# A two-layer SSM, Fourier and attention backbone: the second layer's rotations go from GpSimd to VectorE

## The chip, the core and the metric

The kernel runs on one core of a Trainium2 chip. The core has TensorE for matmuls (PE in the profile), VectorE (DVE), ScalarE (ACT), GpSimd (POOL) and SyncE (SP), each with an instruction queue of its own that it works off in order; they meet through semaphores. Measured is the time of one execution on the device, in microseconds (us); a kernel's time is the median of its runs.

## What is computed

Two layers; each mixes 512 latent tokens and 256 context tokens by three heads side by side (a complex state-space model, a Fourier mixer, a windowed attention with rotary embedding), with one projection in and one out, and then runs a gated FFN. Cut to what the change touches:

```python
h = modulate(rmsnorm(x, g_pre_mix), sh1, sc1) @ w_in
u, f, q, k, v = jnp.split(h, splits, axis=-1)
y_ssm, yc_ssm = s5_mixer(u, uc, ...)       # for both directions: h_t = lam * h_(t-1) + B u_t, lam complex
y_fft = fnet_mixer(f, w_fourier)
q = axial_rope(q); k = axial_rope(k)       # x1*cos - x2*sin, x2*cos + x1*sin
y_na = na_latent(q, k, v, kc, vc, rpb)
o = jnp.concatenate([y_ssm, y_fft, y_na], axis=-1) @ w_out
x = x + g1 * rmsnorm(o, g_post_mix)
x = x + g2 * rmsnorm(swiglu(modulate(rmsnorm(x, g_pre_ffn), sh2, sc2), ...), g_post_ffn)
```

## The kernel before

Almost all of the time is matmuls in split precision: a float32 operand is cut into a high part (a copy on ACT, L584) and a low part (a subtraction on DVE, L565), and three products are summed (L593, L641, L859, L864, L1181). The stages of a layer follow each other; inside the mixing stage they are woven.

**The state-space stage.** `ssm` runs twelve steps k (six groups of heads, two directions each). Step k has two halves. `ssm_scan` multiplies the step's input by a table on PE (L725, four matmuls into PSUM), turns the result by a rotation on DVE (three products and a sum, L280, read from PSUM), runs four real scans on DVE (L735), and turns the result back: three products with the cosine and sine parts of the step's table (L738 to L740), a small memset (L743 or L746), and a difference (L744 in even steps, L747 and L748 in odd ones). `ssm_out` multiplies the outcome on PE (L760, and L762 in odd steps, which close a group) and applies a GELU by ACT and DVE (L283, whose output tile is `z`). L757 opens the PSUM tile of a group. The table `tab` of a step has three buffers; the table of step k+3 is loaded (L507, from SP's queue) once step k's last product, L740, has read its own. In the first layer the tables are built while the stage runs; in the second they are loaded ready-made.

**What is woven with it.** The chunks of the input projection (L593), named u0 to u2, k0, q0, k1, q1, k2, q2, f0, f1; each q and k chunk goes through `rope`: a copy by ACT (L697), a shuffle on DVE (L698), a product with the sine table (L699), a product with the cosine table and a sum (L280 on the `s` tiles). Then the values' projection (L641) and the Fourier mixer (L849, L859, L864). After the last step the attention starts (`attn`, first scores on PE at L985): it loads keys (L936) and queries (L935) through DMAs on POOL's queue. The queries go into a buffer `u` that held tables of the state-space steps, so this load waits for the last `ssm_out` matmul (L762); the keys go into `tab` buffers. The softmax's first step on DVE is L1006.

**What sets the order.** The program is written as generators that are woven in fixed ratios. The framework then schedules: it assigns every instruction a place in its engine's queue, by its own estimate of when operands and buffers are ready. An instruction that goes to another engine therefore also moves its neighbours, on PE and in the DMA queue too.

In the first layer (`l == 0`) the products with the sine table and the turning back run on DVE, in the second on POOL.

Of the kernel before, what the change touches and what calls it, by code (L numbers as in the profile page):

```python
# [12 lines left out]
ALU = mybir.AluOpType  # L13
# [21 lines left out]
class Builder:  # L35
# [654 lines left out]
    def rope(self, l, dst, pl, pc, scale):  # L690
        nc = self.nc
        if self.rc is None:
            self.rc, self.rs = self.s(), self.s()
            nc.sync.dma_start(self.rc, self.ap["rope"][:, 0, :])
            nc.sync.dma_start(self.rs, self.ap["rope"][:, 1, :])
        q, sh = self.s(), self.s()
        nc.scalar.activation(q, pl, AF.Copy, scale=scale)  # L697
        nc.vector.stream_shuffle(sh, q, [(i + 16) % 32 for i in range(32)])  # L698
        (nc.vector if l == 0 else nc.gpsimd).tensor_tensor(out=sh, in0=sh, in1=self.rs, op=ALU.mult)  # L699
        self.tt(q, q, self.rc, ALU.mult)  # L700
        self.tt(q, q, sh, ALU.add)
        parts = [(q, 0, NL)]
        if pc is not None:
            qc = self.c()
            nc.scalar.activation(qc, pc, AF.Copy, scale=scale)
            parts.append((qc, NL, NT))
        for x, a, b in parts:
            new = self.s if a == 0 else self.c
            hl = (new(F32R), new(F32R))
            self.split(*hl, x)  # L710
            for i in range(2):
                nc.sync.dma_start(dst(i)[..., a:b], hl[i].bitcast(F32))


    def ssm_scan(self, l, k, tab):
        nc = self.nc
        u, d = k // 2, k % 2
        U = self.U[u // 2]
        tab = tab[0]
        bT = tab[:, 0:512].rearrange("p (g c) -> p g c", g=4)  # L720
        co = tab[:, 512:896].rearrange("p (g c) -> p g c", g=4)
        si = tab[:, 896:1280].rearrange("p (g c) -> p g c", g=4)
        sp = self.ps("a", [128, 4, 96])
        for i in range(4):
            nc.tensor.matmul(sp[:, i, :], bT[:, i, :], U[:, 4 * (u % 2) + i, 32 * d:32 * d + 96],  # L725
                             start=True, stop=True)
        src = sp if d == 0 else sp[:, :, ::-1]
        t1, t2, gg = (self.q(shape=(128, 4, 96)) for _ in range(3))
        self.tt(t1, src, co, ALU.mult)
        self.tt(t2[0:64], src[64:128], si[64:128], ALU.mult)  # L730
        self.tt(t2[64:128], src[0:64], si[0:64], ALU.mult)
        self.tt(t1, t1, t2, ALU.add)
        for i in range(4):
            j = k * 4 + i
            nc.vector.tensor_tensor_scan(gg[:, i, :], self.rho[l][:, j:j + 1].to_broadcast([128, 96]),  # L735
                                         t1[:, i, :], 0.0, op0=ALU.mult, op1=ALU.add)
        gp = nc.vector if l == 0 else nc.gpsimd
        gp.tensor_tensor(out=t1, in0=gg, in1=co, op=ALU.mult)  # L738
        gp.tensor_tensor(out=t2[0:64], in0=gg[64:128], in1=si[64:128], op=ALU.mult)
        gp.tensor_tensor(out=t2[64:128], in0=gg[0:64], in1=si[0:64], op=ALU.mult)  # L740
        hh = gg
        if d == 0:
            gp.memset(hh[:, :, 0:1], 0.0)  # L743
            gp.tensor_tensor(out=hh[:, :, 1:96], in0=t1[:, :, 0:95], in1=t2[:, :, 0:95], op=ALU.subtract)  # L744
        else:
            gp.memset(hh[:, :, 31:32], 0.0)  # L746
            gp.tensor_tensor(out=hh[:, :, 32:96], in0=t1[:, :, 94:30:-1], in1=t2[:, :, 94:30:-1], op=ALU.subtract)  # L747
            gp.tensor_tensor(out=hh[:, :, 0:31], in0=t1[:, :, 30::-1], in1=t2[:, :, 30::-1], op=ALU.subtract)  # L748
        return hh
# [703 lines left out]
```

## Time and profile before

| | us |
|---|---|
| median of the 3 runs shown | 1658.99 |
| lowest and highest of them | 1652.31, 1659.48 |
| the profiled execution | 1655.93 |
| its span, first to last instruction | 1654.1 |
| PE busy | 1588.4 (96%) |
| DVE busy | 996.6 (60%) |
| POOL busy | 237.2 (14%) |
| second layer's state-space stage, from first L725 to first L985 | 1060.87 to 1171.64 |

The profile is one execution. Each row of its views gives times from the start of the span. "Idle before" is the time for which an engine had nothing to run ahead of an instruction, and the arrow names what ended it. A busy PE is not a PE at its peak; its granted clock is given beside it, 1.00 for 2.4 GHz and 0.50 for 1.2 GHz.

### The profile page before, as it was taken

To read this page: it belongs to the slowest core of one execution; us is meant where nothing else is said; L and a number is where in the kernel's file an instruction comes from. 1 tells how busy PE (TensorE), PEld (TensorE's weight loads), DVE (VectorE), ACT (ScalarE), POOL (GpSimd) and SP (SyncE) were. 2 spreads that over 40 slices of the span, in tenths; PEclk is the share of its full clock that TensorE was granted. 3 is DMA by queue.
4 is the path that set the end of the run, shared out by engine and by line. 5 is a ranking of instruction groups with operands and counts; after the bars stand their busy time and mean duration, and the time that the engine had idled before them with its cause. 6 is when DMAs were issued, how large, how long until landed. Compare 5 with 4: busy or idle time off the path is not lost. (4 is left out here: it accounts for less than half of the span.)

```text
span 1654.1 us, 23548 instructions
## 1 busy us (share of the span) xinstructions
PE 1588.4 (96%) x9097; PEld 1305.8 (79%) x9097; DVE 996.6 (60%) x1891; ACT 651.9 (39%) x1241; POOL 237.2 (14%) x266
## 2 busy tenths in 40 slices
PE   5999689999999999999999999989999999999997
PEld 1887676678988888778788788879777888888886
DVE  7699986765565666433343357697764534554455
ACT  6546545646556322211121138322554432222222
POOL 1000022002111224000000014375411100000002
PEclk8999899999999999999999999999899999999999
DMA  8444377634133424632524356476724422233222
GB/s 319 157 151 137 93 213 240 234 129 166 58 126 117 147 92 140 218 142 90 191 99 149 126 185 207 159 227 198 222 65 140 133 87 100 77 119 103 84 80 86
DMA packets 101391, 240.08 MB, mean 145 GB/s; under 512 B 25424, under 2 KB 56784, under 8 KB 88480
## 3 DMA queue, kind: packets, MB, share of 16 engines
q1 hardware_dynamic: 97968, 229.93, 41.3%
q0 software_dynamic: 3312, 8.65, 1.7%
q8 instruction: 71, 1.16, 0.3%
q14 instruction: 40, 0.33, 0.1%
HBM read 201.26 MB, written 38.47 MB: 145 GB/s over the span
## 5 line engine op out<-in xcount | busy, mean ns | idle before, releaser
L593 PE MATMUL b<-s,wh 128*128 128x512 f32 (+1 forms) x1856 | 551.0, 376 | 1.6 <-DVE s L565 0.6
L593 PEld LDWEIGHTS b<-s,wh 128*128 128x128 f32 x1856 | 337.8, 189 | 74.5 <-issue 9.8
L593 PE MATMUL b<-s,wl 128*128 128x512 f32 (+1 forms) x928 | 345.8, 374 | 1.6 <-DVE wl L565 1.6
L584 ACT ACTIVATE wh<-wr 128x1024 fp32r<-128x1024 f32 (+4 forms) x184 | 185.3, 1027 | 341.8 <-PE b L593 248.2
L565 DVE TENSOR_TENSOR wl<-wr,wh 128x1024 fp32r<-128x1024 f32 (+4 forms) x184 | 221.1, 1217 | 110.0 <-ACT wh L584 100.4
L280 DVE TENSOR_TENSOR q<-q,b 128x512 f32<-128x512 f32 x180 | 122.7, 684 | 165.6 <-PE b L1181 165.0
L593 PEld LDWEIGHTS b<-s,wl 128*128 128x128 f32 x928 | 175.0, 189 | 32.8 <-DVE wl L565 2.7
L593 PE MATMUL b<-c,wh 128*128 128x256 f32 x944 | 179.1, 284 | 0.0
L593 PEld LDWEIGHTS b<-c,wh 128*128 128x128 f32 x944 | 151.3, 191 | 5.5 <-issue 0.6
L283 DVE SCALAR_TENSOR_TENSOR s<-s,b 128x512 f32<-128x512 f32 x88 | 60.2, 685 | 134.2 <-PE b L593 87.0
L1181 PE MATMUL b<-wh,tab 128*128 128x512 f32 x400 | 136.9, 393 | 0.0
L593 PE MATMUL b<-c,wl 128*128 128x256 f32 x472 | 133.1, 284 | 0.0
L1181 PE MATMUL b<-wh,s 128*128 128x512 f32 x384 | 130.0, 392 | 0.0
L593 PEld LDWEIGHTS b<-c,wl 128*128 128x128 f32 x472 | 90.2, 191 | 1.4 <-issue 0.2
L1181 PEld LDWEIGHTS b<-wh,tab 128*128 128x128 f32 x400 | 75.0, 188 | 19.2 <-ACT c L1158 2.5
L1181 PEld LDWEIGHTS b<-wh,s 128*128 128x128 f32 x384 | 72.1, 188 | 19.9 <-issue 2.5
L1181 PE MATMUL b<-wl,tab 128*128 128x512 f32 x200 | 78.3, 392 | 0.0
L1181 PE MATMUL b<-wl,s 128*128 128x512 f32 x192 | 74.7, 390 | 0.0
L1213 POOL TENSOR_TENSOR q<-q,g 128x512 f32<-128x512 f32 x10 | 13.9, 1392 | 367.0 <-ACT junk L515 336.1
L584 ACT ACTIVATE s<-s 128x512 fp32r<-128x512 f32 x43 | 26.9, 627 | 92.2 <-DVE s L283 52.8
L527 POOL TENSOR_TENSOR ss<-ss,cols 128x1 f32<-128x1 f32 x42 | 30.3, 723 | 191.4 <-DVE ss L283 190.7
L1158 ACT ACTIVATE s<-b 128x512 f32<-128x512 f32 x44 | 25.9, 589 | 78.1 <-PE b L593 78.1
(325 smaller groups left out, 2615.6 us busy)
## 6 DMA issues: line engine op xcount, KB each, us to landing
wr<-in_w_gu SPq DMA_DIRECT2D x44, 1024.0 KB
wmod<-in_w_mod SPq DMA_DIRECT2D x46, 512.0 KB
wr<-in_w_down SPq DMA_DIRECT2D x22, 1024.0 KB
wmod<-in_w_mod SPq DMA_DIRECT2D x16, 1024.0 KB
wr<-in_w_in SPq DMA_DIRECT2D x10, 1024.0 KB
u<-in_w_mod SPq DMA_DIRECT2D x18, 512.0 KB
wr<-in_w_out SPq DMA_DIRECT2D x8, 1024.0 KB
tab<-tabd SPq DMA_DIRECT2D x12, 640.0 KB
```

The costliest lines, as they stand in the source:

```text
L280: self.nc.vector.tensor_tensor(out=out, in0=a, in1=b, op=op)
L283: self.nc.vector.scalar_tensor_tensor(out=out, in0=a, scalar=s, in1=b, op0=op0, op1=op1)
L527: nc.gpsimd.tensor_tensor(out=ss[:, 3:4], in0=ss[:, 2:3], in1=self.mhalf, op=ALU.pow)
L565: (eng or self.nc.vector).tensor_tensor(out=lo, in0=x, in1=hi.bitcast(F32), op=ALU.subtract)
L584: ins = self.nc.scalar.activation(hi, x, AF.Copy)
L593: self.nc.tensor.matmul(out, a[k], h[k][v][:, cs], start=(k == 0 and i == 0), stop=(k == 7 and i == 2))
L1158: nc.scalar.activation(tmp[v], gp, AF.Tanh, scale=0.5)
L1181: nc.tensor.matmul(pd, a[v][:, cs], w[:, ds], start=(j == 0 and i == 0), stop=(j == n - 1 and i == 2))
L1213: (nc.gpsimd, nc.vector)[hf].tensor_tensor(out=oo[hf], in0=oo[hf], in1=gates[t // 4][:, hf * 512:(hf + 1) * 512], op=ALU.mult)
```

## The change

Two expressions that choose the engine by the layer now choose VectorE in both. In the second layer six instructions of L699 and the twelve steps' L738, L739, L740, the memsets L743 or L746, and L744 or L747 and L748, move from POOL's queue to DVE's. What they compute, their tiles and the tiles' pools stay as they were.

```diff
@@ rope
-        (nc.vector if l == 0 else nc.gpsimd).tensor_tensor(out=sh, in0=sh, in1=self.rs, op=ALU.mult)
+        (nc.vector).tensor_tensor(out=sh, in0=sh, in1=self.rs, op=ALU.mult)
@@ ssm_scan
-        gp = nc.vector if l == 0 else nc.gpsimd
+        gp = nc.vector
         gp.tensor_tensor(out=t1, in0=gg, in1=co, op=ALU.mult)
         gp.tensor_tensor(out=t2[0:64], in0=gg[64:128], in1=si[64:128], op=ALU.mult)
         gp.tensor_tensor(out=t2[64:128], in0=gg[0:64], in1=si[0:64], op=ALU.mult)
```

The scheduler gives new places to the instructions around them, from the second layer's first steps up to the attention's first scores; behind that the queues are as before.

DVE, the last scan (k = 11, `q<-rho`) and what follows it up to the attention's first softmax step; `wl` are weights' low parts, 128x1024 those of the output projection, `c<-wr` those of the FFN. Before:

```order
L565 TENSOR_TENSOR wl<-wr,wh 128x768
L735 SCALAR_TENSOR_TENSOR q<-rho_146,q 128x96 x4
L565 TENSOR_TENSOR wl<-wr,wh 128x384
L283 SCALAR_TENSOR_TENSOR z<-q,b 128x384
L565 TENSOR_TENSOR s<-b,s 128x512 x4
L565 TENSOR_TENSOR c<-b,c 1x256
L565 TENSOR_TENSOR c<-wr,c 128x256 x3
L283 SCALAR_TENSOR_TENSOR q<-q,b 128x384
L565 TENSOR_TENSOR c<-wr,c 128x256 x2
```

And now:

```order
L565 TENSOR_TENSOR wl<-wr,wh 128x1024
L565 TENSOR_TENSOR c<-wr,c 128x256
L565 TENSOR_TENSOR wl<-wr,wh 128x1024
L283 SCALAR_TENSOR_TENSOR z<-q,b 128x384
L735 SCALAR_TENSOR_TENSOR q<-rho_146,q 128x96 x4
L738 TENSOR_TENSOR q<-q,tab 128x384
L739 TENSOR_TENSOR q<-q,tab 64x384
L740 TENSOR_TENSOR q<-q,tab 64x384
L746 MEMSET q 128x4
L747 TENSOR_TENSOR q<-q 128x4x64
L748 TENSOR_TENSOR q<-q 128x4x31
L565 TENSOR_TENSOR s<-s,u 128x512
```

The last scan has moved behind the Fourier mixer's splits (`s<-b,s`), the FFN's and two of the output projection's, and the turning back stands behind it on the same queue.

PE, from the last matmuls of the state-space stage to the first scores; L864 are 30 matmuls of the Fourier mixer. Before:

```order
L760 MATMUL b<-q,u 128x96
L762 MATMUL b<-U,q 128x96
L864 MATMUL b<-wh,s 128x260 x2
L864 MATMUL b<-wl,s 128x260
...
L864 MATMUL b<-wh,c 128x260 x2
L864 MATMUL b<-wl,c 128x260
L985 MATMUL b<-tab,u 128x256 x30
```

And now:

```order
L864 MATMUL b<-wh,c 128x260 x2
L864 MATMUL b<-wl,c 128x260
L757 LDWEIGHTS zero
L757 MATMUL b<-zero 128x384
L760 MATMUL b<-q,u 128x96 x5
L762 MATMUL b<-U,q 128x96
...
L760 MATMUL b<-q,u 128x96
L762 MATMUL b<-U,q 128x96
L985 MATMUL b<-tab,u 128x256 x24
```

The 30 matmuls stood between the last step's L762 and the first scores; now they stand ahead of the last two steps' `ssm_out`, and the scores follow L762 at once.

## Rows read from the trace of the kernel before

**Rows 1.** The page: busy time by engine; costliest groups (busy us, mean ns, idle before).

```profile
PE 1588.4 (96%) x9097; PEld 1305.8 (79%) x9097; DVE 996.6 (60%) x1891; ACT 651.9 (39%) x1241; POOL 237.2 (14%) x266
...
L584 ACT ACTIVATE wh<-wr 128x1024 fp32r<-128x1024 f32 (+4 forms) x184 | 185.3, 1027 | 341.8 <-PE b L593 248.2
L565 DVE TENSOR_TENSOR wl<-wr,wh 128x1024 fp32r<-128x1024 f32 (+4 forms) x184 | 221.1, 1217 | 110.0 <-ACT wh L584 100.4
```

**Rows 2.** PE's waits from 1030 to 1240: us in total, times, longest.

```profile
PE b L760 <- POOL q L748: 3.2, 2, 2.4
PE b L725 <- DVE z L283: 2.2, 1, 2.2
```

**Rows 3.** Busy us (and instructions) of each engine by stretch, PE's clock, DMA share.

```profile
1052.00:1170.00 118.00, 110.93 (x667) 99.16 (x668) 99.18 (x177) 33.41 (x69) 72.30 (x82) 0.97 0.73 228
...
1120.00:1164.00 44.00, 42.11 (x275) 40.02 (x275) 29.49 (x60) 12.30 (x25) 25.32 (x35) 1.00 0.68 217
1060.00:1120.00 60.00, 54.83 (x311) 46.99 (x310) 57.21 (x95) 14.40 (x26) 41.17 (x40) 0.94 0.78 242
```

**Rows 4.** PE's timeline: start us, us, instruction, idle before it.

```profile
1164.82 0.35 PE L760 MATMUL b<-q,u 128*128 128x96 f32 x2
...
1170.64 0.28 PE L864 MATMUL b<-wl,c 1*128 1x260 f32 x1
1171.64 0.98 PE L985 MATMUL b<-tab,u 64*128 64x256 f32 x12 [0.72 <-DMA u<-qd]
1174.35 4.19 PE L985 MATMUL b<-tab,u 64*128 64x256 f32 x18 [1.73 <-DVE am L1006]
```

**Rows 5.** The query loads of L935: POOL's timeline, and issue to landing of all six.

```profile
1166.82 1.43 POOL L935 DMA_DIRECT2D u<-qd  x2 [2.40 <-PE b L762]
...
DMA to landing us min/median/max: 4.7/5.4/7.5
```

**Rows 6.** DVE's groups, 80 to 236 (first layer), columns as in group 1.

```profile
L735 DVE TENSOR_TENSOR_SCAN q<-rho,q 128x96 f32<-128x96 f32 x48 | 13.4, 336 | 0.0
...
L280 DVE TENSOR_TENSOR s<-s 128x512 f32<-128x512 f32 x12 | 8.2, 686 | 0.0
...
L738 DVE TENSOR_TENSOR q<-q,tab 128x384 f32<-128x384 f32 x12 | 6.6, 553 | 0.1
L280 DVE TENSOR_TENSOR q<-q 128x384 f32<-128x384 f32 x12 | 6.6, 551 | 0.1
...
L699 DVE TENSOR_TENSOR s<-s 128x512 f32<-128x512 f32 x6 | 4.1, 685 | 0.0
L744 DVE TENSOR_TENSOR q<-q 128x380 f32<-128x380 f32 x6 | 3.3, 547 | 0.0
...
L565 DVE TENSOR_TENSOR c<-c 128x256 fp32r<-128x256 f32 x6 | 2.5, 418 | 0.0
L747 DVE TENSOR_TENSOR q<-q 128x256 f32<-128x256 f32 x5 | 2.1, 420 | 0.0
...
L748 DVE TENSOR_TENSOR q<-q 128x124 f32<-128x124 f32 x5 | 1.4, 282 | 0.0
```

**Rows 7.** DVE's groups, 1050 to 1165 (second layer, POOL turning).

```profile
L735 DVE TENSOR_TENSOR_SCAN q<-rho,q 128x96 f32<-128x96 f32 x48 | 17.3, 418 | 0.2
L280 DVE TENSOR_TENSOR s<-s 128x512 f32<-128x512 f32 x12 | 13.6, 1134 | 2.5 <-POOL s L699 2.3
...
L280 DVE TENSOR_TENSOR q<-q 128x384 f32<-128x384 f32 x12 | 9.2, 770 | 0.1
...
L565 DVE TENSOR_TENSOR c<-c 128x256 fp32r<-128x256 f32 x3 | 4.0, 1321 | 0.0
```

**Rows 8.** POOL's groups, 1050 to 1165 (second layer), the first of nine that move.

```profile
L738 POOL TENSOR_TENSOR q<-q,tab 128x384 f32<-128x384 f32 x12 | 14.2, 1185 | 31.7 <-issue 19.0 <-DVE q L735 9.1 <-PE b L762 2.7
```

**Rows 9.** Stretches of 4 us, columns as in group 3: two late ones.

```profile
1176.00:1180.00 4.00, 3.90 (x19) 3.68 (x20) 3.42 (x14) 2.76 (x7) 0.76 (x2) 0.50 0.97 356
...
1188.00:1192.00 4.00, 4.00 (x39) 3.13 (x38) 2.80 (x8) 2.49 (x6) 2.17 (x3) 1.00 0.65 155
```

## The prediction

> **What bounds the kernel now.** I read the page's busy times first. PE is busy for 96% of the span, DVE for 60%, POOL for 14% [rows 1], so over the whole kernel only what lets PE wait can move the time. That average hides the stage in question. Next I looked for waits of PE around the second layer's state-space stage. Only 3.2 us in two waits are for POOL's turning back, L748, and one wait of 2.2 us is for a GELU on DVE [rows 2]. So what the change can remove directly is small. Third, the stage as a whole. From 1052 to 1170 PE is busy for 110.9 of 118 us at a mean clock of 0.97, and DVE for 99.2 us. DVE's load is uneven: 57.2 of 60 us up to 1120, but only 29.5 of 44 us from 1120 to 1164 [rows 3]. DVE is nearly full where POOL is to hand its work over, and has some 15 us free after that. Last, how the stage ends: the last L760 and L762 start at 1164.8, the queries' load is issued at 1166.8 because it had waited for them, the Fourier matmuls (L864) run until 1170.9, and the first scores start at 1171.6, after a wait of 0.7 us for that load [rows 4, 5]. The attention thus starts when three things are done: the last state-space step, the load behind it, and PE's other work. The question is which of them is last after the change.
>
> **Part 1: what DVE gets.** The first layer runs the same instructions on DVE with POOL idle, so their prices are known [rows 6]. The rows of L739 and L740 there read like L738's. 36 products of 0.553 are 19.9 us; 6 of L699 at 0.685 are 4.1; 6 of L744 at 0.547, 6 of L747 at 0.42 and 6 of L748 at 0.282 are 7.5; the twelve memsets, the smallest of the groups, I take as under 1 us together. The sum is 32 us. On a full engine an independent instruction starts a little before the last one's end, so some of the 66 cost less. I estimate 3 us off, from the first layer's DVE, where rows that add up to more than the time they lie in stand side by side. DVE is loaded with 29 to 32 us.
>
> **Part 2: what DVE gets back.** Instructions that DVE keeps take longer while POOL turns. The scan takes 336 ns in the first layer and 418 in the second, the sums and products on `s` tiles 686 and 1134, the sum on `q` tiles 551 and 770, the split on `c` tiles 418 and 1321 [rows 6, 7]. Times their counts this is 48 x 0.082 = 3.9, 12 x 0.448 = 5.4, 12 x 0.219 = 2.6 and 3 x 0.903 = 2.7: 14.6 us. Other splits are lengthened as well, by less. I take 15 to 18 us back. POOL's instruction of 1.2 us for what DVE does in 0.55 [rows 6, 8] is thus paid for on DVE too, to a good part. Net, DVE's queue in this stage grows by 11 to 17 us.
>
> **Part 3: what is moved.** By the new order the last scan stands behind two 128x1024 splits of the output projection, 1.2 us each [rows 1], that were done after it. So ahead of the stage's end DVE has 99 + 14 + 2.4 = 115 to 116 us of work, against 118 us in which it used to be done. It doesn't fit with much to spare: DVE can't start step 0 before PE has multiplied its input (about 1 us lost), and even in its fullest stretch it is idle for 2.8 of 60 us [rows 3]. Before, POOL's last turning was done by 1164.8, when PE read it [rows 4]. I put the end of the last turning on DVE at 1167.5, with 1165 (all overlaps good, 18 us given back) and 1171 (none) as bounds.
>
> On PE, the last matmuls of the stage take 1.9 us (from 1164.8 to the start of L864 in the trace), and from the queries' load to the scores it was 1171.6 - 1166.8 = 4.8 us [rows 4, 5]; the loads of this line land after 4.7 to 7.5 us. Until now 30 Fourier matmuls covered it. Now they stand ahead of the last `ssm_out`, and nothing is left in PE's queue that could cover it. So the scores start at 1167.5 + 1.9 + 4.8 = 1174.2, where they started at 1171.6: 2.6 us later, with bounds of 0 and 6. What is given back: after the first scores PE waited another 1.73 us for the softmax [rows 4], since DVE still had splits to do. In the new order these are done, and DVE is free when the scores come; I take 0.6 to 1 us off. **Sum: +2 us.**
>
> The two waits for POOL and the one for the GELU [rows 2] don't enter this sum. They vanish or not, PE then comes earlier to the last steps and waits there for DVE. That is where the 5.4 us go: from the middle of the stage to its end. POOL itself has nothing queued behind these instructions but the key and query loads; with an empty queue it issues the keys as soon as their buffers are free, and the queries still wait for L762. SP's queue waits for L740 before each table load; on DVE that product ends no later than on POOL in the first steps, and the table has 6 us or more before PE needs it. I cost that at nothing; a table that comes late would cost what PE waits for it, 1 to 2 us, once or twice, ahead of an end that DVE sets.
>
> PE's clock is 0.50 in the stretch at 1176 and 1.00 again at 1188, after the idle time around the first scores [rows 4, 9]. With the new order PE is idle there for longer, three times in a row (for the GELU ahead of L757, for the last turning, for the load). The low clock should begin earlier, partly in time in which PE waits anyway, and end about as long after the scores as now: 0 to 3 us more. I take it as nothing and keep the 3 for the range.
>
> **The rivals.** *Faster: DVE was held back by more than its lengthened rows show.* For this speaks that POOL is busy for 72 us in this stage [rows 3], of which I let DVE get back only 15 to 18. If it gets back 30 us or more, its queue shrinks in net, the steps are ready before PE asks for them, and PE sets the end. Its idle time in the stage, 7 us, and the clock's 3% of 111 us would be gone: 10 us earlier. Against it speaks that the lengthened rows are the direct measure, and that DVE's work can't end much before 1165 by the sum of its instructions. The time would be 1649. The Trainium skill (SBUF — State Buffer, Who interferes with whom) holds that a VectorE instruction with two SBUF inputs and a GpSimd instruction that reads SBUF exclude each other for a whole instruction, whichever starts first. Taken at its full length that would give back nearly all of POOL's time, and the end would be PE's, as in this rival; the lengthened rows show a quarter of it.
>
> *Slower: PE is the late one, and the last scan is caught behind it.* On DVE the last scan stands behind the output projection's splits, and these need ring buffers that the Fourier matmuls (L864) read last. If PE reaches the end of L864 late, everything behind is one chain: a split on ACT (1.0), two on DVE (1.2 each) [rows 1], the GELU (0.5), four scans (1.1), the turning (2.4) [rows 6], the last matmuls (1.9), the load (4.8) [rows 4, 5]: 14 us. It decides from the point where L864 ends later than about 1160. Without waits PE would be there at 1157. If PE loses as much time on the way as it does now, by waits for DVE in place of those for POOL, it is there at 1168 (it ends L864 at 1170.9 now, with the last 2.9 us of `ssm_out` ahead of it). The scores then start at 1182, 10 us later: 1669, and with more of the low clock 1671. For it speaks DVE's 95% load up to 1120. The Trainium skill (Perfetto Trace Analysis, Optimizing Scalar/DVE Operations) holds that work may be moved off a saturated VectorE, even to GpSimd, which this change does the other way round; it adds that moving between the two may not help, since they share a port. Against it speaks that the scheduler has put the early `ssm_out` matmuls further back among the projection's, so PE should find them ready.
>
> **How the numbers follow.** The profiled execution took 1655.93 us, with a span of 1654.1; +2 makes it 1658. The median of the runs is 3 us above that execution, and the runs spread over 7 us. Against the median I predict 1661, with 1657 to 1665 for this case alone. It has a chance of 0.66, the slower rival 0.24, the faster one 0.10. A measurement of this kernel can tell about 0.5%, 8.3 us, from no change, so the first case is "the same", and the rivals are on either side of that bound, the slower one just beyond. The range takes in most of the slower rival and half the way to the faster: 1653 to 1670.
>
> **What would show it.** Right: in the changed kernel the scan takes about 336 ns again and the sums on `s` tiles 686; DVE is busy for over 110 us of the 118; no wait of PE for POOL is left in the stage, and the longest waits stand at its end, for DVE ahead of the last L757 and L760 and for the queries' load ahead of L985, about 5 us; the first scores start at 1173 to 1176. Wrong: first scores before 1168 (DVE had been held back by more), or after 1179, with L864 ending after 1160 (PE late, the chain of 14 us). A stage that ends as predicted with a total off by more than 5 us would mean that the difference lies elsewhere, in the clock or in the attention.

## The result, and the profile after

The changed kernel takes 1667.71 us (median of 7 runs, 1663.91 to 1676.33), the kernel before 1658.99 (7 runs): a ratio of 1.0063, 95% interval 1.0045 to 1.0080. That is 0.6% slower, some 10 us, just beyond the 0.5% that the prediction named as the least that can be told from no change. The page of the profiled execution answers to [rows 1]:

```profile
PE 1597.2 (96%) x9097; PEld 1314.2 (79%) x9097; DVE 1007.0 (60%) x1963; ACT 652.6 (39%) x1241; POOL 168.5 (10%) x194
```

POOL has 68.7 us less to do, DVE only 10.4 us more. The span is 1667.9 us, against 1654.1, but not all of the difference belongs to the change. The first L725 of the second layer, ahead of which nothing was changed, comes at 1065.28 instead of 1060.87 (the last section shows that this goes with the clock of the first layer). I therefore measure the **stage**, from that L725 to the first L985: 120.55 us (1065.28 to 1185.83), where it was 110.77. What follows the first L985 takes 482.1 us, where it took 482.5. So all of the change's cost, 9.8 us in the trace, lies in the stage. PE's waits there answer to [rows 2]; columns are us in total, times, longest. The first line is one more of the kernel before, which [rows 2] lacks (there PE waited for the GELU ahead of L757 too); the others are the changed kernel's:

```profile
PE b L757 <- DVE z L283: 1.5, 2, 0.9
...
PE b L985 <- DMA u<-qd: 4.3, 1, 4.3
PE b L757 <- DVE z L283: 4.0, 1, 4.0
PE b L725 <- DMA tab<-tabd: 2.9, 1, 2.9
PE b L859 <- DVE s L565: 2.2, 1, 2.2
PE b L760 <- DVE q L748: 0.9, 1, 0.9
PE b L985 <- DVE am L1006: 0.9, 1, 0.9
```

The waits for POOL are gone, and longer ones have come. When they came is seen if the stage is cut into its first 60 us, the next 30 and the rest. The kernel before (columns as in group 3: PE, PEld, DVE, ACT and POOL busy, PE's clock, DMA share, GB/s):

```profile
1060.90:1120.90 60.00, 54.83 (x315) 47.15 (x314) 56.87 (x94) 15.01 (x28) 41.11 (x41) 0.94 0.78 243
1120.90:1150.90 30.00, 29.17 (x188) 28.00 (x188) 21.05 (x43) 5.44 (x14) 17.15 (x23) 1.00 0.60 178
1150.90:1171.60 20.70, 18.96 (x134) 17.21 (x132) 15.15 (x31) 12.53 (x27) 12.26 (x20) 1.00 0.88 283
```

The changed kernel, and its whole stretch that answers to the first of [rows 3]:

```profile
1065.30:1125.30 60.00, 60.00 (x362) 54.02 (x361) 58.30 (x130) 18.00 (x34) 0.00 (x0) 1.00 0.79 243
1125.30:1155.30 30.00, 27.08 (x169) 25.87 (x169) 24.32 (x60) 7.78 (x14) 0.00 (x0) 0.94 0.65 199
1155.30:1185.80 30.50, 19.08 (x106) 16.96 (x106) 22.87 (x53) 8.79 (x19) 6.00 (x11) 0.70 0.71 238
...
1052.00:1170.00 118.00, 112.89 (x678) 102.50 (x677) 108.58 (x242) 37.57 (x70) 1.18 (x2) 0.96 0.72 226
```

This table is the result in short. In the first 60 us the change does what one would wish: PE is never idle (60.00 us, where it was 54.83), at the full clock. But PE's work in the stage is a fixed amount. What it did early was taken from what used to cover the last state-space steps, which depend on each other through DVE. These did not come earlier; the last step's L760 starts 112.5 us into the stage (1177.76 less 1065.28), where it started after 104.0 us (1164.82 [rows 4] less 1060.87). In the last part PE is busy for 19.08 of 30.5 us, at a mean clock of 0.70; before it was 18.96 of 20.7 at the full clock. Up to 1155 PE was ahead; for the rest it needed 9.8 us more.

How the time goes from 1125 on, first in PE's timeline (start us, us, instruction, count, idle before it):

```profile
1132.56 1.31 PE L725 MATMUL b<-U,tab 128*128 128x96 f32 x8 [2.92 <-DMA tab<-tabd]
...
1158.14 6.32 PE L859 MATMUL b<-s 128*128 128x256 f32 x29 [2.19 <-DVE s L565]
...
1170.11 0.28 PE L864 MATMUL b<-wl,c 1*128 1x260 f32 x1
1174.36 0.50 PE L757 MATMUL b<-zero 1*128 1x384 bf16 x1 [3.97 <-DVE z L283]
...
1177.76 0.74 PE L760 MATMUL b<-q,u 128*128 128x96 f32 x2 [0.95 <-DVE q L748]
...
1185.83 1.65 PE L985 MATMUL b<-tab,u 64*128 64x256 f32 x12 [4.35 <-DMA u<-qd]
```

and in DVE's, with the two rows of ACT that prepare the splits of the output projection (128x1024):

```profile
1146.98 0.97 DVE L565 TENSOR_TENSOR wl<-wr,wh 128x780 fp32r<-128x780 f32 x1 [5.08 <-ACT wh L584]
...
1164.08 0.69 DVE L565 TENSOR_TENSOR s<-b,s 128x512 fp32r<-128x512 f32 x1 [0.92 <-ACT s L584]
...
1169.04 1.06 ACT L584 ACTIVATE wh<-wr 128x1024 fp32r<-128x1024 f32 x1 [0.76 <-PE b L864]
1170.32 1.05 ACT L584 ACTIVATE wh<-wr 128x1024 fp32r<-128x1024 f32 x1
...
1171.14 1.23 DVE L565 TENSOR_TENSOR wl<-wr,wh 128x1024 fp32r<-128x1024 f32 x1
...
1172.61 1.23 DVE L565 TENSOR_TENSOR wl<-wr,wh 128x1024 fp32r<-128x1024 f32 x1
1173.74 0.56 DVE L283 SCALAR_TENSOR_TENSOR z<-q,b 128x384 f32<-128x384 f32 x1
1174.21 1.11 DVE L735 TENSOR_TENSOR_SCAN q<-rho,q 128x96 f32<-128x96 f32 x4
...
1177.42 0.28 DVE L748 TENSOR_TENSOR q<-q 128x124 f32<-128x124 f32 x1
```

Step 8's table comes 2.9 us late (1132.56). DVE stands idle for 5.1 us ahead of a split of the Fourier weights (1146.98), for ACT's half of it. PE waits 2.2 us for a Fourier split, and its 29 L859 then take 6.32 us, where they took 3.67, since they run at the half clock.

From 1146.98 to the end of the last turning at 1177.70, DVE is busy for 29.3 of 30.7 us, and its one wait in them is the 0.92 us at 1164.08. So it is DVE's queue that says when the last scan starts. L864 ends at 1170.4, but the two splits of the output projection do not wait for it: ACT's halves are done by 1170.10 and 1171.37, and DVE comes to its own at 1171.14 and 1172.61, without idle time. The last GELU, the last scan and the turning stand behind them, the last L760 starts at 1177.76, and the queries' load stands bare behind it.

So the 9.8 us have two parts. The last L760 starts 8.5 us later in the stage. From there to the first scores it is 8.1 us instead of 6.8: the last matmuls run at the half clock and let the load go out 1.6 us later after their start (3.6 instead of 2.0), and the load takes 0.3 us less.

### The profile page after: what moved, and what is told of

The parts are those of the page before. It is cut to its first block, busy times and chain, and to the rows that moved or that the text cites. A ratio compares the mean times of both kernels' runs of the same rounds, so it can differ in the third digit from the quotient of the medians.

```text
span 1667.9 us, 23502 instructions
## 1 busy us (share of the span) xinstructions
PE 1597.2 (96%) x9097; PEld 1314.2 (79%) x9097; DVE 1007.0 (60%) x1963; ACT 652.6 (39%) x1241; POOL 168.5 (10%) x194
## 5 line engine op out<-in xcount | busy, mean ns | idle before, releaser
L163 PE MATMUL b<-wmod,scT 128*32 128x512 f32 x192 | 40.3, 691 | 17.8 <-DVE sm L277 9.3
L985 PE MATMUL b<-tab,u 64*128 64x256 f32 x312 | 46.8, 327 | 5.3 <-DMA u<-qd 4.3
```

What stands on the lines that cost most here:

```text
L163: nc.tensor.matmul(acc[32 * j:32 * j + 32, :], self.scT[:, k, :], w[:, j, :], start=(k == 0), stop=(k == 7))
L985: self.nc.tensor.matmul(sp[e], q[r, a, qs], k[r, b, ks], start=(n == 0), stop=(n == 2))
```

## The experiments

Three places could be the cause: the end's order (last scan behind the output projection's splits, load uncovered), DVE's idle wait ahead of the Fourier weights, and the late table. The rival to all three is plain load: DVE has 10 us more to do, and that shows somewhere. "Rest" is the time from the first L985 to the end of the span; the next column is stage plus rest against the kernel before (593.2 us), and the last the timed ratio with its interval.

| kernel | stage us | rest us | against before | ratio |
|---|---|---|---|---|
| before | 110.8 | 482.5 | 0 | |
| the change | 120.5 | 482.1 | +9.4 | 1.0063 (1.0045 to 1.0080) |
| e1: L699 alone | 111.9 | 483.2 | +1.8 | 1.0009 (0.9989 to 1.0029) |
| e2: turning alone | 121.4 | 484.4 | +12.6 | 1.0083 (1.0053 to 1.0113) |
| e3: change, cover | 116.2 | 480.1 | +3.1 | 1.0037 (1.0019 to 1.0054) |
| e5: steps 6 to 11 alone | 113.9 | 482.1 | +2.8 | 1.0000 (0.9981 to 1.0019) |
| e7: change, hold | 120.2 | 482.6 | +9.6 | 1.0059 (1.0036 to 1.0083) |
| e8: change, cover, hold | 116.9 | 480.2 | +3.9 | 1.0039 (1.0016 to 1.0062) |
| e9: L699 alone, cover | 115.3 | 482.2 | +4.3 | 1.0027 (1.0012 to 1.0043) |
| e10: change, GELU writes by POOL | 118.3 | 488.7 | +13.7 | 1.0083 (1.0059 to 1.0107) |
| e17: change, cover, SP relieved | 113.4 | 481.4 | +1.6 | 1.0009 (0.9990 to 1.0029) |
| e18: L699, steps 0 to 5, cover | 114.6 | 480.4 | +1.8 | 1.0031 (1.0014 to 1.0048) |
| e19: change, cover, products left out | 105.1 | 481.2 | -6.9 | 0.9955 (0.9939 to 0.9970) |
| e21: e17, q and k splits on POOL | 115.4 | 481.3 | +3.5 | 1.0022 (0.9999 to 1.0046) |

The trace's column and the timed one (0.001 is 1.7 us) agree within 3.4 us everywhere, so both are of use. A difference below that is not read from either as one of time; where two traces are compared below, it is to see at which place the time went. Each trace is one execution.

### e3: the end's order put back

```diff
@@ ssm_out
-                nc.tensor.matmul(yp[:, i, :], tab[2][:, i, :], U[...], ...)
+                self.last = nc.tensor.matmul(yp[:, i, :], tab[2][:, i, :], U[...], ...)
@@ fnet, second layer only
-                three(pn, ...)
+                self.behind(self.last, three, pn, ...)
```

> The changed kernel, with one order imposed: the second layer's 30 Fourier matmuls (L864) come after the last state-space matmul (L762) in TensorE's queue, and so lie again between it and the first scores, as in the kernel before. All instructions stay on the engines the change gave them; the last scan moves ahead of the output projection's splits on VectorE. Theory (the order at the end costs the 9 us: queries' load uncovered, last scan behind the splits): the wait of L985 for the queries' load falls from 4.3 us to under 1.5, the wait of 4.0 us ahead of L757 to under 2, the first scores start 6 to 10 us earlier within the stage (stage of 111 to 115 us, where the changed kernel has 120.5), ratio to the kernel before 0.999 to 1.002. Rival (VectorE's added load of 10 to 16 us is the cost, wherever it shows): the waits only move, stage 118 to 121 us, ratio 1.004 to 1.008.

Measured: 1.0037, a stage of 116.2 us. Its waits:

```profile
PE b L757 <- DVE z L283: 6.6, 1, 6.6
...
PE b L985 <- DMA u<-qd: 0.5, 1, 0.5
```

The load's wait went as expected, and the last scan no longer stands behind the output projection's splits; the stage is 4.3 us shorter, the rest 2.0. But the wait of L757 grew from 4.0 to 6.6 instead of shrinking. L757 opens the last group's PSUM tile, for which the GELU of the group before must be done; nothing but that GELU stands between the two groups now. By the times the repair is worth 4 of the 10 us, with intervals that overlap a little, and neither theory covers all of it.

Where the gain lies is seen if the stage is cut at the last L760. It starts 107.7 us into the stage (1173.98), 4.8 us earlier than in the changed kernel. From there to the first scores it is 8.5 us, where it was 8.1: L864 now fills the time in which PE had waited for the load, and the covered load saved nothing. The 4.8 us come from DVE. From the split at which it had stood idle to the last scan it takes 23.3 us (1147.15 to 1170.44) instead of 27.2: 3.0 of work that now stands behind the scan, and the wait of 0.92 at 1164.08, which is gone. And the idle time ahead of that split is 0.8 us shorter. So the order is worth some 3 us here. The wait at 1164.08 went with the clock: e3's 29 L859, behind the same wait of 2.2 us, took 3.92 us at the full clock. So they did in e10, which has the changed kernel's order there.

### e1, e2, e5: parts of the change alone

e1 and e2 each take one of the two changed lines back: e1 keeps only L699 on DVE, e2 only the turning back. e5 keeps the turning back of the later steps:

```diff
@@ ssm_scan, in the kernel before
-        gp = nc.vector if l == 0 else nc.gpsimd
+        gp = nc.vector if l == 0 or k >= 6 else nc.gpsimd
```

> The kernel before with only the six products with the sine table (L699) moved to VectorE; the turning back stays on GpSimd. VectorE gets 4.1 us, less than 3 net. But the scheduler, as in the full change, then puts the 30 L864 ahead of the last ssm_out and the last scan behind one of the output projection's splits on VectorE. Theory (order): first scores as late as with the full change or later, since the last turning is now slower on GpSimd (some 5 us instead of 2.4): L985 waits over 3 us for the queries' load, stage 117 to 123 us, ratio 1.004 to 1.009. Rival (VectorE's load): no change, stage 110 to 113 us, ratio 0.999 to 1.002.

> The kernel before with only the turning back (L738 to L748) moved to VectorE; L699 stays on GpSimd. The scheduler again puts L864 ahead of the last ssm_out; the last scan stands ahead of the output projection's two splits, its L746 to L748 behind them. Theory (order): the queries' load uncovered again (L985 waits 3 to 5 us), the last turning caught behind the splits, ratio 1.003 to 1.007, a stage of 115 to 120 us. Rival (VectorE's load): 28 of 32 us moved, so nearly the full cost, ratio 1.004 to 1.007; the two agree here. Second rival (L699, which two of VectorE's own steps wait for, is where the cost arises): ratio 0.999 to 1.001.

> The kernel before with only the turning back of steps 6 to 11 moved to VectorE; steps 0 to 5 and L699 stay on GpSimd. VectorE gets about 14 us where it was least busy (29 of 44 us from 1120 to 1164 before). In the schedule the last ssm_out stands ahead of all Fourier matmuls L859 and L864, so the queries' load is covered. Theory (order): no cost, the queries' load hidden (L985 waits under 1 us), ratio 0.998 to 1.002, stage 109 to 113 us; if the last ssm_out now waits for VectorE early, with 54 matmuls queued behind it, up to 3 us more. Rival (VectorE's load): half of the full cost, ratio 1.002 to 1.004.

Measured: 1.0009, 1.0083, 1.0000; e2 lies above, and e5's stage of 113.9 us just outside, what was expected. So L699 is not the source: alone it costs nothing that can be measured, and the turning without it costs as much as the whole change. Of the turning, steps 6 to 11 alone cost nothing that can be measured.

e1 brought my theory down in its simple form. (Its expectation is wrong in one point: in e1's queue the last scan stands ahead of the output projection's splits.) Its stage ends uncovered, and PE waits for the queries as in the changed kernel:

```profile
PE b L985 <- DMA u<-qd: 4.9, 1, 4.9
```

and still the stage is 111.9 us. PE's waits for POOL had shrunk from 3.2 to 0.8 us, those for the GELU (L725 and L757) from 3.7 to 0.3. An exposed load of 4.9 us at the end is thus no cost by itself: the last L760 starts at 105.0 us into the stage, and from there to the scores it is 6.9 us, as before the change (6.8), when L864 covered the load.

### e7, e8: DVE's idle wait

```diff
@@ wload, for the second layer's Fourier weights only
-                self.split(hi, lo, raw[:, a:b])
+                self.behind(self.scan9, self.split, hi, lo, raw[:, a:b])
```

`scan9` is step 9's last scan. e8 has e3's edit as well.

> The changed kernel, with the two splits of the Fourier weights (L565, 128x780 and 128x520) placed behind step 9's last scan on VectorE instead of ahead of step 9's rotation. In the changed kernel VectorE stood idle for 5.1 us ahead of the first of them, with step 9's work ready behind it. TensorE's order stays as in the changed kernel but for four L859, and the queries' load stays uncovered. Theory (that idle time made the last three steps late): step 9's and step 10's outputs come 3 to 5 us earlier, L859's wait of 2.2 us and the half clock after it go, stage (first L725 to first L985) 114 to 117 us where the changed kernel has 120.5, ratio to the kernel before 1.001 to 1.004. Rival (VectorE is simply full, its idle time only moves): stage 119 to 121 us, ratio 1.005 to 1.008.

> Both repairs of the order: the Fourier matmuls L864 behind the last state-space matmul, and the Fourier weights' splits behind step 9's last scan. All work stays on the engines that the change gave it. Theory (the cost is order, in two places): stage 110 to 113 us, as before the change, L757's wait for the GELU under 3 us where the first repair alone left 6.6; ratio 0.998 to 1.001. Rival (VectorE's load is the cost of what the first repair leaves): stage 115 to 117 us, ratio 1.003 to 1.005.

Measured: 1.0059 and 1.0039, as without the hold (1.0063 and 1.0037). The hold did not take the idle time away, it moved it, as the rival said. In e7 DVE was idle for 4.3 us at the same place, now for ACT's square of the GELU, and PE waited at the end instead:

```profile
PE b L760 <- DVE q L748: 6.5, 1, 6.5
PE b L985 <- DMA u<-qd: 5.9, 1, 5.9
```

The last scan came early (1171.0, where the changed kernel had 1174.2), but the turning behind it waited for the two splits of the output projection. What the 5.1 us would be worth if DVE had work for them, e7 does not show; e10 and e17 do below.

### e9: e1 with its load covered

The edit is e3's, made in e1.

> Only L699 on VectorE, the turning back on GpSimd, and the Fourier matmuls L864 behind the last state-space matmul. L699 alone on VectorE left the time as it was, with a wait of 4.9 us for the queries' load at the end of the stage. Theory (that wait is a price of its own, and the same in every kernel that ends the stage so): the wait falls under 1 us, stage 107 to 109 us where it was 111.8, ratio 0.996 to 0.999. Rival (the last step is then late by GpSimd's turning, which L864 had covered): L760 waits 3 to 5 us for L748, stage 111 to 112 us, ratio 1.000 to 1.002.

Measured: 1.0027, a stage of 115.3 us: worse than either theory, and nearer the rival. PE's timeline:

```profile
1172.19 0.59 PE L760 MATMUL b<-q,u 128*128 128x96 f32 x2 [2.61 <-POOL q L748]
...
1183.92 1.65 PE L985 MATMUL b<-tab,u 64*128 64x256 f32 x12 [3.90 <-DMA u<-qd]
```

With L864 no longer ahead of it, L760 waits 2.6 us for POOL's turning. That is not the loss: it starts at 103.6 us into the stage, 1.4 us earlier than in e1. But the last matmuls run at the half clock, and the load, issued at 1175.64, lands only 8.3 us later, where e1's took 4.8 and the changed kernel's 4.5 (1181.35 to 1185.83). Why it took longer I didn't settle; a keys' load (L936) was issued 3.6 us before it, but in the changed kernel one was issued 3.8 us before. So the repair that goes with a gain of 4 us in one kernel goes with a stage 3.5 us longer in another (by the times 3 us, with intervals that overlap).

### e10 and e17: the late table

The table of step 8 uses the buffer that step 5's L740 frees. In the changed kernel that L740 ended at 1125.4, and SP's queue was not ready (issue times of the DMAs):

```profile
1115.63 6.48 SPq L663 DMA_DIRECT2D U<-ud  x8
1122.20 4.08 SPq L776 DMA_DIRECT2D zd<-z  x8
...
1126.87 0.38 SPq L507 DMA_DIRECT2D tab<-tabd  x1
```

e10 issues L776 from POOL's queue in the second layer. e17 issues all of it but the last pair's, and L663 of the third pair, from POOL, and has e3's edit.

> The changed kernel, with the second layer's writes of the GELU's output (L776, eight DMAs for each of three pairs of groups) issued from GpSimd's queue, which the change left nearly empty, instead of SyncE's, where 4.1 us of them stood ahead of step 8's table. TensorE's and VectorE's orders stay as in the changed kernel. Theory (the late table, 2.9 us of TensorE's time, is passed on to the end): that wait falls under 0.5 us, stage 116 to 118.5 us, ratio 1.002 to 1.005. Rival (TensorE comes earlier and waits for VectorE by as much): stage 119 to 121 us, ratio 1.005 to 1.008.

> The changed kernel with the Fourier matmuls L864 behind the last state-space matmul, and SyncE's queue relieved ahead of step 8's table: the third group pair's eight U loads (L663) and the first two pairs' writes of the GELU's output (L776) are issued from GpSimd's queue. The last pair's writes stay with SyncE, since from GpSimd they stood between the softmax's masks and cost 6 us. TensorE's order is that of the first repair alone (ratio 1.0037, stage 116.3 us). Theory (a late table adds a part of its own): the wait for it falls under 0.5 us, stage 113 to 115 us, ratio 1.001 to 1.003. Rival (VectorE's turning of step 5, which frees the table's buffer, is late, and SyncE is not what matters): the wait stays at 1.5 us or more, or TensorE waits later by as much, stage 115.5 to 117 us, ratio 1.003 to 1.005.

In e10 PE's idle time ahead of step 8's L725 fell from 2.9 to 1.45 us (the profile puts what is left down to no DMA), and the stage shrank by 2.3 us. But the rest grew by 6.6: the last pair's writes now stood between the softmax's masks on POOL.

```profile
1177.96 2.08 POOL L997 TENSOR_TENSOR q<-c,rb 128x256 f32<-128x256 f32 x3
1180.00 4.23 POOL L776 DMA_DIRECT2D zd<-z  x8
```

e17 has the orders of e3 on PE and on DVE, row for row, so against e3 only the places of these DMAs differ: 1.0009 instead of 1.0037, a stage of 113.4 us instead of 116.2. The table is issued at 1120.02, the moment L740 ends, and PE no longer waits for it. The same three parts of the stage:

```profile
1059.90:1119.90 60.00, 60.00 (x361) 54.00 (x360) 58.31 (x130) 17.99 (x34) 6.90 (x14) 1.00 0.81 253
1119.90:1149.90 30.00, 27.69 (x184) 26.11 (x184) 28.65 (x70) 7.78 (x14) 6.32 (x12) 1.00 0.69 203
1149.90:1173.30 23.40, 15.86 (x94) 14.28 (x92) 15.84 (x41) 7.58 (x18) 5.39 (x10) 0.71 0.80 253
```

With all of the change's work on DVE, two repairs, neither of which takes work off DVE, bring the time so near to that of the kernel before that the two can't be told apart. The interval of e17 and that of e3 overlap, so the times alone do not show the second repair. The traces show how the late table is passed on. DVE's row of the split at which it stood idle, in e3, e10 and e17:

```profile
1147.15 0.97 DVE L565 TENSOR_TENSOR wl<-wr,wh 128x780 fp32r<-128x780 f32 x1 [4.31 <-ACT wh L584]
...
1142.41 0.97 DVE L565 TENSOR_TENSOR wl<-wr,wh 128x780 fp32r<-128x780 f32 x1 [3.61 <-ACT wh L584]
...
1137.19 0.97 DVE L565 TENSOR_TENSOR wl<-wr,wh 128x780 fp32r<-128x780 f32 x1 [0.70 <-ACT wh L584]
```

| us | the change | e10 | e3 | e17 |
|---|---|---|---|---|
| PE idle ahead of step 8's L725 | 2.92 | 1.45 | 2.14 | 0 |
| DVE idle ahead of this split | 5.08 | 3.61 | 4.31 | 0.70 |
| from the split's start to the last scan's | 27.2 | 26.2 | 23.3 | 23.3 |
| last L760 starts, from the stage's start | 112.5 | 110.0 | 107.7 | 104.1 |
| first scores, from the stage's start | 120.5 | 118.3 | 116.2 | 113.4 |

In the first three DVE is idle for 2.16 or 2.17 us more than PE had waited for the table. PE comes to the values' projection (L641) later by that wait, ACT's half of the split waits for L641, and DVE for ACT. So the late table and DVE's idle time are not two places but one: e17 is without the one and nearly without the other, and its last L760 starts 3.6 us earlier in the stage than e3's. It starts where that of the kernel before did (104.0), with 32 us of work more on DVE. What is left of e17's longer stage lies behind it, where PE ran at 0.50 of its clock (9.2 us to the first scores, 6.8 before).

So the last step was late, in these traces, by some 5 us of idle time on DVE, most of it from a late table, by 0.9 for L859 at the half clock, and by 3 us of work that the new order had put ahead of the last scan. Not shown is whether the relief of SP's queue would make the kernel before faster as well; that was not run.

### e18, e19: the load itself

e18 is e5's mirror: L699 and steps 0 to 5 on DVE, with e3's edit. e19 is e3 without the twelve rotary products of the second layer (part of the rotary embedding is not computed).

> L699 and the turning back of steps 0 to 5 on VectorE, steps 6 to 11 on GpSimd, and the Fourier matmuls L864 behind the last state-space matmul: the other half of the run with steps 6 to 11 on VectorE, which cost nothing (ratio 1.000). Theory (VectorE is full in the stage's first 60 us, so what is put there makes the later steps late): as slow as the changed kernel with the same repair, stage 115 to 118 us, ratio 1.003 to 1.006. Rival (VectorE's load counts wherever it is put, by its amount): half of that, stage 112.5 to 114.5 us, ratio 1.000 to 1.003.

> The changed kernel with the Fourier matmuls behind the last state-space matmul, and with the twelve rotary products of the second layer (the six with the sine table, L699, and the six with the cosine table) left out, so that part of the rotary embedding is not computed: VectorE has 8.2 us less to do, all of it in the stage's first 60 us; TensorE and the DMAs have the same work. The scheduler then puts the last ssm_out ahead of all but the last Fourier matmuls, as in the kernel before. Theory (VectorE's load in the first 60 us is what the first repair left): stage 109 to 113 us, ratio 0.997 to 1.001. Rival (it isn't the load): stage 115 to 117 us, ratio 1.003 to 1.005.

e18: 1.0031, 114.6 us. The ratio is the theory's, the stage just outside the rival's; against e5 (1.0000) the timed intervals touch, and the trace's sums (+1.8 and +2.8) don't tell the two apart. That the early half is the dear one is thus not shown.

e19: 0.9955. With 8.2 us less on DVE the stage is 11.1 us shorter than e3's, and stage and rest are 7 us shorter than the kernel before's, more than the theory said. The last 15 us of its stage are full again:

```profile
1156.00:1171.10 15.10, 14.10 (x86) 12.52 (x86) 11.57 (x28) 7.00 (x17) 5.05 (x9) 0.77 0.82 249
```

So less on DVE can end the stage earlier. That it is the load and not the order isn't shown: the scheduler also put the last group's first matmuls ahead of L859 again, as in the kernel before, and no wait for a table is left, so load, order and table aren't parted here.

### e21: other work for the idle POOL

```diff
@@ rope, in e17
-            self.split(*hl, x)
+            self.split(*hl, x, nc.gpsimd if l == 1 else None)
```

> The changed kernel with L864 behind the last state-space matmul and SyncE's queue relieved (ratio 1.0009, stage 113.4 us), and with other work given to the now idle GpSimd: the second layer's nine splits of the rotated queries and keys (L565 in the rotary helper, 6 of 128x512, 3 of 128x256), for which no instruction of VectorE waits, only their writes to memory. VectorE has 5.4 us less to do in the first 60 us, at the rows' lengths, less what GpSimd's some 10 us of work lengthen its other instructions by (estimated 2 to 3 us from the kernel before). Theory (VectorE's load early in the stage is paid for nearly one to one, as when the rotary products were left out): 2 to 5 us faster than without this step, stage 108 to 111 us, ratio to the kernel before 0.996 to 0.999. Rival (what VectorE gets back goes to the lock with GpSimd, or the keys' and queries' writes come late): stage 112 to 114 us, ratio 1.000 to 1.002.

Measured: 1.0022, 115.4 us: outside both ranges. DVE was busy for 3.1 us less than in e17 (1003.8 and 1006.9), and nothing of it shows in the time. The table's wait is back, though SP issued it the moment L740 ended (1123.37): it was needed 4.6 us later and took 7.5 to come, where e17's was there within 4.4. None of the kernels that compute everything beats the kernel before; the nearest are e1, e5 and e17, which can't be told from it (e21's interval just reaches it).

## Why the prediction was right or wrong

The range held the time, but the likeliest case (+2 us) did not happen. By the prediction's own signs it was wrong: first scores after 1179 and L864 ending after 1160, in the kernel before's time. The slower rival's number came true, and its mechanism only in part, so the range held partly by luck.

- **Part 1, what DVE gets:** right. The moved instructions took what the first layer's rows said: 36 x 0.553 + 6 x (0.690 + 0.547 + 0.420 + 0.282) = 31.5, with the memsets 32 us. (They are not 66: DVE's count rises by 72. The sum does not use that number.) The rows that answer to [rows 6, 7], from 1054 to 1180, are:

```profile
L735 DVE TENSOR_TENSOR_SCAN q<-rho,q 128x96 f32<-128x96 f32 x48 | 13.3, 341 | 0.0
L280 DVE TENSOR_TENSOR s<-s 128x512 f32<-128x512 f32 x12 | 8.2, 684 | 0.1
L280 DVE TENSOR_TENSOR q<-q 128x384 f32<-128x384 f32 x12 | 6.7, 554 | 0.1
L738 DVE TENSOR_TENSOR q<-q,tab 128x384 f32<-128x384 f32 x12 | 6.7, 554 | 0.2
...
L699 DVE TENSOR_TENSOR s<-s 128x512 f32<-128x512 f32 x6 | 4.1, 690 | 0.1
...
L565 DVE TENSOR_TENSOR c<-c 128x256 fp32r<-128x256 f32 x3 | 1.3, 422 | 0.0
```

- **Part 2, what DVE gets back:** right in kind (341 ns for the scan, 684 and 554 for the sums, 422 for the split) and in size: the durations of the instructions that stayed on DVE add up to 15.9 us less, and 15 to 18 were predicted. DVE's busy time grew by only 10.4 us, below the 11 to 17, because neighbours in the fuller queue overlap by some 6 us more, where I took 3 off. 15.9 us are a quarter of the 68.7 us by which POOL's busy time fell. The Trainium skill (SBUF — State Buffer, Who interferes with whom) holds that a VectorE instruction with two SBUF inputs contends with a GpSimd instruction that reads SBUF, and that the lock is exclusive. Taken over POOL's whole instructions, as the prediction took it, nearly all of the 68.7 would have come back; this trace doesn't agree with it taken so.
- **Part 3, the last turning:** this is the step that failed. I put its end at 1167.5, from the sum of DVE's work as if it were packed from the stage's start. It ended at 1177.7; less the 4.4 us by which this execution was late already, 1173.3, and the bounds were 1165 to 1171. The sum was not too small: from 1056.4 (1052 in this execution's time) to 1177.7 DVE was busy for 111.9 us, where I had 115 to 116. What I left out is the time for which DVE has nothing it may run, 9.4 us there, of which 5.08 lie ahead of the Fourier weights' split and 0.92 at 1164.08.
- **The late table:** costed at nothing, since "an end that DVE sets" would hide 1 to 2 us. It was 2.9 us, and it is the larger part of those 5.08: the end that DVE sets came later by it. I had not looked at what stands ahead of it on SP's queue: L663 and L776, 10.6 us of issues, kept it 1.5 us past its buffer's release.
- **The last matmuls:** a term of 1.9 us (to the end of the last L762; to the start of L864 it is 1.7). They took 3.7, at the half clock.
- **The queries' load:** right: 4.35 us of waiting, 4.5 from its issue to the scores. **Given back at the softmax:** right, 0.9 us of waiting instead of 1.73 [rows 4]. **The early waits that vanish** [rows 2]: right, PE is busy for 60.00 of the first 60 us, and the gain went to the end, as the text said; but the end cost more than the gain.
- **The clock:** costed at 0 to 3 us. That the low clock behind the first scores would end about as long after them as before was right: the rest of the kernel did not grow. But it came in the stage as well, behind the wait for the table (0.66 in the 4 us from 1132), in L859, which lost 2.65 us by it (6.32 instead of 3.67), and from the last group's L757 on:

```profile
1160.00:1164.00 4.00, 4.00 (x20) 3.61 (x20) 3.06 (x7) 1.15 (x2) 0.55 (x1) 0.50 1.04 410
...
1196.00:1200.00 4.00, 4.00 (x23) 3.01 (x23) 2.25 (x6) 1.41 (x3) 0.72 (x1) 0.50 0.32 95
```

- **The slower rival:** PE did come late to L864, and its numbers held: 15.4 us from the end of L864 to the first scores (14 predicted), scores at 1185.8, or 1181.4 in the kernel before's time (1182 predicted). But its chain is not what the trace shows. The output projection's splits did not wait for L864; they and the last scan waited in DVE's queue. In e10, with the same order, L864 ended 3.9 us earlier in the stage (1163.4), and the last L760 started only 2.5 us earlier, as much as DVE's idle time had shrunk. **The faster rival** fell: DVE got back less than POOL's time, and its queue grew in net.

## What to carry to other kernels

Where an engine works through a fixed amount, time gained in the middle of a stage is spent at its end if a serial chain ends the stage: ask what covers the last steps once the cover has been used up earlier. An engine's end is its work and the time for which the head of its queue has to wait: adding up loads gives only the first. When a change reorders queues, read the end's order before adding up loads: here the same load cost 10 us in the scheduler's order, and nothing that could be measured with the end's order and the table's place in SP's queue put right. A transfer "needed only later" is hidden by slack that the change may itself remove; look at what else its queue issues in the 10 us ahead.

## What the runs showed of the hardware

The first layer's clock is not the same in every execution, and the time at which the second layer's stage starts goes with it. The stretch from 200 to 300, the same code in all kernels, in the changed kernel and in e2:

```profile
200.00:300.00 100.00, 90.91 (x652) 66.67 (x652) 69.97 (x177) 50.85 (x117) 19.61 (x29) 0.91 0.66 202
```

```profile
200.00:300.00 100.00, 91.05 (x567) 66.13 (x567) 62.78 (x161) 44.75 (x100) 18.71 (x28) 0.81 0.60 181
```

At 0.96 (the kernel before) the second layer's stage started at 1060.9, at 0.91 at 1065.3, at 0.81 at 1074.5. The change moved the time by less than that, so the spans of two profiled executions can't be compared here. Times between two marks of the trace can, with care: the 29 L859, behind the same wait of 2.19 us, took 6.32 us in the changed kernel and 3.91 in e10, which has the same order there, as the granted clock was 0.50 in the one and 1.00 in the other.

From its issue to PE's use, a load of one table (L507) took under 4.4 us in e17, 5.7 in the changed kernel (1126.87 to 1132.56) and 7.5 in e21, and the query load 4.5 to 8.3. With lead times of that size, and a spread whose cause these runs do not show, an issue that is 1.5 us late can decide whether PE waits.
